# Column tiles with both high parts before both low parts, smaller memory claims and a shorter LayerNorm path in a two-layer hybrid trunk

## The chip, the cores and the metric

The kernel runs on one core of one Trainium2 chip. The metric is device time in microseconds (us), the median over several executions. Engines are named as in the profile: PE is TensorE (matmuls), PEld its weight load, DVE VectorE, ACT ScalarE, POOL GpSimd, SP the engine that issues most DMAs.

## What is computed

Two layers over 256 tokens of width 2048, then a final RMSNorm. Each layer normalises, projects to 14,848 columns at once, runs four token mixers of width 512 on their columns, and merges them:

```
h = rms_norm(x, norm_g)
proj = h @ w_in
ya = a_bg * depthwise_conv(a_cg * a_x, conv_a_w) * silu(a_z)          # A: 3 taps
yb = gqa_attention(axial_rope(rms_norm(q)), axial_rope(rms_norm(k)), v) * silu(b_z)   # B
yc = rwkv7_bidir(h, c_r, c_k, c_v, ...) * silu(c_z)                    # C: scan, both directions
u  = depthwise_conv(d_val * sigmoid(d_gate), dw_w) + dw_b              # D: 31 taps
yd = silu((u - mean(u)) * rsqrt(var(u) + LN_EPS) * ln_g + ln_b) * silu(d_z)
bp = einsum('bskc,kcd->bskd', stack([ya, yb, yc, yd]), w_branch)
x  = x + sum(sigmoid(gates + b_gate) * bp, branches) @ w_out
```

All arithmetic is float32. On PE a weight and an activation are each split into a rounded high part and a rest (low part), and a product is made of three passes: high x high, high x low and low x high.

## The kernel before

**Weights.** Per layer 306 chunks of 128x1024 float32 (512 KB) are streamed from memory into four `raw` buffers, one DMA each. From a chunk ACT makes its high part, `hi` (a rounding copy, `fetch`, line 423; three buffers), and DVE its low part, `lo` = raw - hi (`low`, line 437; two buffers). `chunk` (line 444) hands a chunk to PE and sees to it that three chunks are ahead in `hi` and two in `lo`; both copies are issued with high priority.

**Column tiles.** `tile_b` (line 478) makes 128 columns of a projection over all 256 tokens from two chunks. The activations stand in slabs as pairs (high | low) of 512 columns, so that one chunk takes 8 matmuls of 128x512 with `hi` (high x high and high x low side by side) and 8 of 128x256 with `lo`. Per chunk `wide` (line 467) issues the 8 with `hi`, then the 8 with `lo`; then comes the second chunk. A layer has 137 such tiles. `tile_branch` (line 488) does the same with one chunk for the branch outputs (32 per layer). Three PSUM buffers (`mg`) hold column tiles, one (`mb`) branch tiles, four (`sd`) the side work.

**Side work.** Normalising and the branches A to D are Python generators that run beside the stream of column tiles. A generator issues a few instructions and yields: a positive number is a delay on the planner's clock `k.now`; a negative one (`MM` -1.0, `PM` -1.5, `LN` -3.6) asks that its next matmul comes so many planner units after its operands are due. After each matmul of a column tile `pump` (line 352) issues the steps that are due, for each generator as far as its lead permits (`LEAD_A` 2.0, `LEAD_B` 1.8, `LEAD_D` 1.0), and so the place of a side matmul among PE's instructions is fixed when the program is built. PE, DVE and ACT each run their instructions in the order in which they were put, and wait where an operand is not there. The order on DVE and ACT is made by a scheduler, which puts `hi` and `lo` first where it can.

**Memory.** Side work takes its buffers from one arena. `room(words)` (line 279) holds a generator back until so many words are free beside what others have claimed. Branch B claims 2900 (line 712), branch C 3300 (line 839), 2400 (line 954) and 4300 (line 980).

**Branch D.** `conv_d` (line 758) adds the 31 taps on DVE, and `branch_d` (line 768) makes the LayerNorm: it adds the four 128-channel parts, sums them over channels on PE (the first sum), subtracts the mean on DVE and squares on ACT per part, adds the four squares, and sums again on PE (the second sum). The first sum is yielded as `LN`, the second as `MM`.

Where the text speaks of a part (`part`, `rounded`), a norm over heads or groups is meant: ACT rounds a value to `part`, DVE puts the rest beside it, and two PE matmuls sum both (`head_rstd`, line 664). Scan chunk means the steps of branch C's recurrence, whose small matrices ACT copies from PSUM (`bdE`, `bdR`, `bdS`).

Of the kernel before, what the change touches and what calls it, by code (L numbers as in the profile page):

```python
# [10 lines left out]
F32 = mybir.dt.float32  # L11
F32R = mybir.dt.float32r
AF = mybir.ActivationFunctionType
# [5 lines left out]
P = 128  # L19
D = 2048  # L20
S = 256
# [188 lines left out]


class Kern:
    AHEAD = 3
    FAR = 1
    INFL = 1.05
    RAW = 9
# [12 lines left out]
    LATE = 3.0  # L229
    LEAD_A = 2.0  # L230
    LEAD_B = 1.8
    LEAD_D = 1.0
    TAP = 1.0
    DMA = 2.5
    SLABS = 9
# [185 lines left out]
        return True  # L421

    def fetch(self):
        nc = self.nc
        while len(self.raws) < 1 + self.FAR and self.load():
            pass
        if not self.raws:
            return False
        raw = self.raws.pop(0)
        hi = self.wtile("hi", 3, F32R)  # L430
        with self.tc.high_priority():
            nc.scalar.activation(hi, raw, AF.Copy)
        self.ready.append([hi, None, raw])
        if self.tiles == 0 and len(self.ready) < 3:
            self.low(self.ready[-1])
        return True

    def low(self, w):

        if w[1] is None:  # L440
            w[1] = self.wtile("lo", 2, F32R)
            with self.tc.high_priority():
                self.nc.vector.tensor_tensor(w[1], w[2], w[0].bitcast(F32), ALU.subtract)

    def chunk(self):
        while len(self.ready) < self.AHEAD and self.fetch():
            pass
        w = self.ready.pop(0)
        self.low(w)
        if self.ready:  # L450
            self.low(self.ready[0])
        return w[:2]


    def passes(self, o, w, xs, first, last):
# [8 lines left out]
            nc.tensor.matmul(o, lo[:, c * P:(c + 1) * P], x[:, 0, :], start=False, stop=last and i == len(xs) - 1)  # L464
            self.pump()

    def wide(self, o, w, xs, first, last):

        nc = self.nc
        hi, lo = w  # L470
        for i, (c, x) in enumerate(xs):
            nc.tensor.matmul(o, hi[:, c * P:(c + 1) * P], x, start=first and i == 0, stop=False)
            self.pump()
        for i, (c, x) in enumerate(xs):
            nc.tensor.matmul(o[:, 0], lo[:, c * P:(c + 1) * P], x[:, 0, :], start=False, stop=last and i == len(xs) - 1)
            self.pump()

    def tile_b(self, src):


        self.tiles += 1
        o = self.psum(*(("mb", 1) if self.tiles == 4 else ("mg", 3))).rearrange("p (a t) -> p a t", a=2)
        for j in range(2):
            w = self.chunk()
            self.wide(o, w, [(k % 8, src[k // 4][:, k % 4]) for k in range(j * 8, j * 8 + 8)], j == 0, j == 1)
        return o

    def tile_branch(self, y):

        ps = self.psum("mb", 1)  # L490
        w = self.chunk()
        for j in range(2):
            self.passes(ps[:, j * S:(j + 1) * S], w, [(j * NT + k, y[:, k]) for k in range(NT)], True, True)
        return ps.rearrange("p (j t) -> p j t", j=2)

    def whole(self, out, ps):
# [196 lines left out]
    def branch_b(self, k, v, qz):  # L693
# [12 lines left out]
        for i in range(NT):  # L706
            while len(qz) <= i:
                yield 0.5
            q, bz = qz[i]
            if i == 0:  # L710
                ys = self.ys[1] = self.operand()
            yield from self.room(2900)
            rs = yield from self.head_rstd(q)
            qr = self.a1()
            yield from self.norm_rope(q, rs, self.pc("qg"), [(slice(0, P), qr)])
            self.f(q, rs)
            pt = self.a([P, 2, 2, S])
            pes = []
            for tb in range(2):
                ps = self.pside()  # L720
                nc.tensor.matmul(ps, qr[:, tb * P:(tb + 1) * P], kz.rearrange("p a t -> p (a t)"),
                                 start=True, stop=True)
                ps2 = ps.rearrange("p (a t) -> p a t", a=2)
                st = self.a([P, 6])
                nc.vector.tensor_reduce(st[:, 0:2], ps2, AX.X, ALU.max)
                nc.vector.tensor_scalar(st[:, 2:4], st[:, 0:2], -0.125, None, ALU.mult)
                pe = self.a([P, 2, S])
                for h in range(2):
                    nc.scalar.activation(pe[:, h], ps2[:, h], AF.Exp, scale=0.125, bias=st[:, 2 + h:3 + h],
                                         accum_out=st[:, 4 + h:5 + h])  # L730
                yield 0.5
                nc.vector.reciprocal(st[:, 4:6], st[:, 4:6])
                for h in range(2):
                    nc.scalar.activation(pe[:, h], pe[:, h], AF.Copy, scale=st[:, 4 + h:5 + h])
                self.f(st)
                pes.append(pe)
                yield 2 * self.MM
            self.f(qr)
            for tb, pe in enumerate(pes):
                ps = self.pside()  # L740
                for h in range(2):
                    for kb in range(2):
                        j = h * 2 + kb
                        nc.tensor.transpose(ps[:, j * P:(j + 1) * P], pe[:, h, kb * P:(kb + 1) * P], self.ident)
                self.f(pe)
                nc.scalar.activation(pt[:, :, :, tb * P:(tb + 1) * P],
                                     ps.rearrange("p (h k t) -> p h k t", h=2, k=2), AF.Copy)
                yield self.MM
            ps = self.pside()
            for kb in range(2):  # L750
                for h in range(2):
                    nc.tensor.matmul(ps[h * 64:h * 64 + 64, :S], vt[:, kb * P + h * 64:kb * P + h * 64 + 64],
                                     pt[:, h, kb, :], start=kb == 0, stop=kb == 1)
            self.f(pt)
            nc.vector.tensor_tensor(bz, ps[:, :S], bz, ALU.mult)
            self.finish(ys, i, bz)
            self.f(bz)
            yield 0.5
# [13 lines left out]
    def branch_d(self, acc, convs, dz):  # L772
# [6 lines left out]
            yield 0.5  # L779
        ys = self.ys[3] = self.operand()  # L780
        yield 0
        sq = self.a([P, NT, S])
        nc.vector.tensor_tensor(sq[:, 0:2], acc[:, 0:2], acc[:, 2:4], ALU.add)
        nc.vector.tensor_tensor(sq[:, 0], sq[:, 0], sq[:, 1], ALU.add)
        yield self.LN
# [1 line left out]
        nc.tensor.matmul(ps[:, :S], self.ones, sq[:, 0], start=True, stop=True)  # L787
        for i in range(NT):
            nc.vector.scalar_tensor_tensor(acc[:, i], ps[:, :S], -1.0 / W, acc[:, i], ALU.mult, ALU.add)
            nc.scalar.activation(sq[:, i], acc[:, i], AF.Square)  # L790
        nc.vector.tensor_tensor(sq[:, 0:2], sq[:, 0:2], sq[:, 2:4], ALU.add)
        nc.vector.tensor_tensor(sq[:, 0], sq[:, 0], sq[:, 1], ALU.add)
        yield self.MM
        ps = self.pside()
        made = nc.tensor.matmul(ps[:, :S], self.ones, sq[:, 0], start=True, stop=True)
        self.f(sq)
# [22 lines left out]
    def rwkv(self, rkv, tl, cz):  # L819
# [5 lines left out]
        for d in range(2):  # L825
# [8 lines left out]
            for p0 in range(0, NT, 2):  # L834
                pp = slice(p0, p0 + 2)
                v5 = lambda x: x.rearrange("p a (c t) -> p a c t", c=NCH)
                while self.cv < p0 + 1:
                    yield 0.5
                yield from self.room(3300)
                lbs = []  # L840
                for i in range(2):
                    lb = self.a([P, 2, P])
# [108 lines left out]
            self.cur.want = 0  # L951

            yield 4.0
            yield from self.room(2400)
            mb = self.a([P, 32, 32])
            for h in range(2):
                for b in range(2):
# [19 lines left out]
            nc.gpsimd.dma_start(scr2[1], xt[:64])  # L977
            self.f(xi, xt)
            self.cur.want = 0
            yield from self.room(4300)  # L980
            bd = self.bd
            ready = []
            self.add(self.inverses(bd, gs, scr2, ready))
# [534 lines left out]
```

## Time and profile before

| | |
|---|---|
| median of 3 runs | 1969.62 us (1969.13 to 1970.98) |
| profiled execution, its own time | 1970.32 us |
| its span (first to last instruction) | 1968.5 us |
| mean granted TensorE clock | 0.992 of full speed |
| PE busy | 1922.6 us (98%) |
| PEld busy | 1705.1 us (87%) |
| DVE busy | 1442.9 us (73%) |
| ACT busy | 1261.6 us (64%) |
| HBM traffic | 173 GB/s over the span |

The shares are averages over the whole span. The waits view lists per engine and operand how long the engine stood idle and which instruction released it; a row of the timeline is a run of like instructions, with its start, the time it took and, in brackets, the idle time before it. In the windows view PEclk is the mean granted clock of a stretch, as a share of full speed. Nearly all instructions bear line 201, the helper that records them; what they are is read from the names of output and inputs.

### The profile page before, as it was taken

To read this page: it belongs to the slowest core of one execution; us is meant where nothing else is said; L and a number is where in the kernel's file an instruction comes from. 1 tells how busy PE (TensorE), PEld (TensorE's weight loads), DVE (VectorE), ACT (ScalarE), POOL (GpSimd) and SP (SyncE) were. 2 spreads that over 40 slices of the span, in tenths; PEclk is the share of its full clock that TensorE was granted. 3 is DMA by queue.
4 is the path that set the end of the run, shared out by engine and by line. 5 is a ranking of instruction groups with operands and counts; after the bars stand their busy time and mean duration, and the time that the engine had idled before them with its cause. 6 is when DMAs were issued, how large, how long until landed. Compare 5 with 4: busy or idle time off the path is not lost.

```text
span 1968.5 us, 32326 instructions
## 1 busy us (share of the span) xinstructions
PE 1922.6 (98%) x12190; PEld 1705.1 (87%) x12190; DVE 1442.9 (73%) x2498; ACT 1261.6 (64%) x2292; POOL 71.3 (4%) x117
## 2 busy tenths in 40 slices
PE   8999999999999999999999999999999999999997
PEld 6888788899988998998888887889899899989886
DVE  7877869967787556666687778699777866565665
ACT  7777577667647776554567766766765577665544
POOL 2001010000001000000000011000001000000000
PEclk9999999999999999999999999999999999999998
DMA  7555453355565445566655555444555544455653
GB/s 256 182 178 171 148 161 136 135 178 184 169 198 171 148 152 190 188 203 215 210 191 182 169 174 165 136 142 151 179 173 186 174 166 151 149 188 195 218 183 128
DMA packets 97692, 343.17 MB, mean 174 GB/s; under 512 B 11808, under 2 KB 12192, under 8 KB 97536
## 3 DMA queue, kind: packets, MB, share of 16 engines
q1 hardware_dynamic: 93312, 331.48, 49.4%
q0 software_dynamic: 3648, 8.59, 1.8%
q8 instruction: 95, 1.56, 0.3%
q10 hardware_dynamic: 576, 1.05, 0.1%
q14 instruction: 61, 0.50, 0.1%
HBM read 332.48 MB, written 8.39 MB: 173 GB/s over the span
## 4 chain that ended last, share of the span: by engine, by line
PE 94%; DVE 4%; ACT 1%; issue 1%; DMA 0%; DVEq 0%; SPq 0%; ACTq 0%
PE mg L201 75%; PE mb L201 9%; PE sd L201 9%; DVE arena L201 2%; DVE lo L201 1%; ACT bdE L201 0%; ACT arena L201 0%; DMA arena<-xT 0%; ACT hi L201 0%; ACT L175 0%; DVE bdE L201 0%; DVE slab L201 0%; DVEq L1513 0%; ACT bdR L201 0%; ACT bdS L201 0%
## 5 line engine op out<-in xcount | busy, mean ns | idle before, releaser
L201 PE MATMUL mg<-slab,hi 128*128 128x512 f32 x4368 | 1135.3, 398 | 11.7 <-DVE slab L201 11.7
L201 DVE TENSOR_TENSOR lo<-raw,hi 128x1024 fp32r<-128x1024 f32 x612 | 748.6, 1223 | 352.2 <-PE mg L201 295.0
L201 ACT ACTIVATE hi<-raw 128x1024 fp32r<-128x1024 f32 x612 | 647.0, 1058 | 472.1 <-PE mg L201 311.8
L201 PEld LDWEIGHTS mg<-slab,hi 128*128 128x128 f32 x4368 | 783.9, 190 | 155.1 <-DVE slab L201 14.9
L201 PEld LDWEIGHTS mg<-slab,lo 128*128 128x128 f32 x4368 | 604.5, 191 | 47.7 <-issue 5.1
L201 PE MATMUL mg<-slab,lo 128*128 128x256 f32 x4368 | 640.3, 286 | 0.0
L201 DVE TENSOR_TENSOR arena<-arena 128x256 f32<-128x256 f32 (+18 forms) x392 | 166.9, 433 | 15.2 <-ACT arena L201 6.9
L201 DVE SCALAR_TENSOR_TENSOR arena<-arena,par 128x256 f32<-128x256 f32 x346 | 154.5, 483 | 4.7 <-ACT arena L201 3.7
L201 PE MATMUL mb<-slab,hi 128*128 128x256 f32 (+1 forms) x1040 | 152.9, 287 | 0.0
L201 DVE TENSOR_TENSOR arena<-mg,arena 128x256 f32<-128x256 f32 x305 | 127.8, 419 | 18.4 <-ACT arena L201 13.2
L201 PEld LDWEIGHTS mb<-slab,hi 128*128 128x128 f32 x1040 | 136.3, 191 | 0.9
L201 ACT ACTIVATE arena<-arena,b_gate 128x256 f32<-128x256 f32 x128 | 64.6, 505 | 73.8 <-DVE arena L201 73.2
L201 ACT ACTIVATE arena<-arena 128x256 f32<-128x256 f32 (+4 forms) x194 | 93.6, 498 | 25.7 <-DVE arena L201 24.8
L201 ACT ACTIVATE arena<-mg 128x256 f32<-128x256 f32 x241 | 89.3, 371 | 6.4 <-PE mg L201 3.7
L201 PE MATMUL mb<-slab,lo 128*128 128x256 f32 x528 | 87.7, 287 | 0.0
L175 ACT ACT_TABLE_LOAD x62 | 79.5, 1283 | 10.2 <-PE sd L201 7.7
L201 DVE SCALAR_TENSOR_TENSOR arena<-arena,mb 128x512 f32<-128x512 f32 x64 | 43.9, 686 | 55.4 <-PE mb L201 45.0
L201 PEld LDWEIGHTS mb<-slab,lo 128*128 128x128 f32 x528 | 73.6, 191 | 0.4
L201 ACT ACTIVATE bdE<-sd 64x128 f32<-64x128 f32 x256 | 62.9, 269 | 8.3 <-PE sd L201 5.8
L201 ACT ACTIVATE arena<-sd 128x64 f32<-128x64 f32 (+4 forms) x122 | 40.0, 330 | 21.9 <-PE sd L201 20.3
L201 ACT ACTIVATE arena<-arena,par 128x256 f32<-128x256 f32 x88 | 42.8, 508 | 5.5 <-DVE arena L201 4.2
L201 PE MATMUL sd<-arena 96*128 96x256 f32 (+3 forms) x224 | 43.7, 338 | 0.0
(96 smaller groups left out, 1019.5 us busy)
## 6 DMA issues: line engine op xcount, KB each, us to landing
raw<-w SPq DMA_DIRECT2D x612, 512.0 KB, 3.3
arena<-xT SPq DMA_DIRECT2D x4, 512.0 KB, 7.5
scratch<-slab POOLq DMA_DIRECT2D x16, 128.0 KB, 3.4
scratch<-arena POOLq DMA_DIRECT2D x8, 256.0 KB, 4.7
arena<-xT SPq DMA_DIRECT2D x8, 256.0 KB, 3.9
x<-arena SPq DMA_DIRECT2D x8, 256.0 KB, 4.8
arena<-x SPq DMA_DIRECT2D x8, 256.0 KB, 3.5
arena<-lorab POOLq DMA_DIRECT2D x16, 96.0 KB, 2.7
```

Of the source, the lines that this page charges most:

```text
L175: return f(out)
L201: return f(out, *args, **kw)
```

## The change

`tile_b` takes both chunks at its start. It issues the 8 matmuls with the first `hi`, the 8 with the second `hi`, then the 8 with the first `lo` and the 8 with the second. Copies for coming chunks are issued at fixed places: a `hi` after the eighth matmul and one at the tile's end, a `lo` after each eight low matmuls, with the DMA of a further `raw` behind it. `wide`, `AHEAD` and the loop in `chunk` go. `LEAD_D` goes from 1.0 to 1.4. The claims of `room` go from 2900 to 2400, 3300 to 3136, 2400 to 2304 and 4300 to 1500. In `branch_d` the buffer of the squares has two parts in place of four, each square is added to the sum as it comes, and the second sum is yielded as `LN`.

```diff
 class Kern:
-    AHEAD = 3
...
-    LEAD_D = 1.0
+    LEAD_D = 1.4
...
     def fetch(self):
-        nc = self.nc
-        while len(self.raws) < 1 + self.FAR and self.load():
-            pass
+
+        nc = self.nc
         if not self.raws:
-            return False
+            return
         raw = self.raws.pop(0)
         hi = self.wtile("hi", 3, F32R)
...
         if self.tiles == 0 and len(self.ready) < 3:
-            self.low(self.ready[-1])
-        return True
-
-    def low(self, w):
-
-        if w[1] is None:
-            w[1] = self.wtile("lo", 2, F32R)
-            with self.tc.high_priority():
-                self.nc.vector.tensor_tensor(w[1], w[2], w[0].bitcast(F32), ALU.subtract)
+            self.low()
+
+    def low(self):
+
+        for w in self.ready:
+            if w[1] is None:
+                w[1] = self.wtile("lo", 2, F32R)
+                with self.tc.high_priority():
+                    self.nc.vector.tensor_tensor(w[1], w[2], w[0].bitcast(F32), ALU.subtract)
+                self.load()
+                return
 
     def chunk(self):
-        while len(self.ready) < self.AHEAD and self.fetch():
-            pass
-        w = self.ready.pop(0)
-        self.low(w)
-        if self.ready:
-            self.low(self.ready[0])
-        return w[:2]
+        return self.ready.pop(0)[:2]
...
     def tile_b(self, src):
...
-        for j in range(2):
-            w = self.chunk()
-            self.wide(o, w, [(k % 8, src[k // 4][:, k % 4]) for k in range(j * 8, j * 8 + 8)], j == 0, j == 1)
+        ws = [self.chunk(), self.chunk()]
+        for k in range(KT):
+            c = k % 8
+            self.nc.tensor.matmul(o, ws[k // 8][0][:, c * P:(c + 1) * P], src[k // 4][:, k % 4], start=k == 0, stop=False)
+            self.pump()
+            if k == 7:
+                self.fetch()
+        for k in range(KT):
+            c = k % 8
+            self.nc.tensor.matmul(o[:, 0], ws[k // 8][1][:, c * P:(c + 1) * P], src[k // 4][:, k % 4, 0, :], start=False,
+                                  stop=k == KT - 1)
+            self.pump()
+            if c == 7:
+                self.low()
+        self.fetch()
         return o
...
     def tile_branch(self, y):
...
             self.passes(ps[:, j * S:(j + 1) * S], w, [(j * NT + k, y[:, k]) for k in range(NT)], True, True)
+        self.low()
+        self.fetch()
         return ps.rearrange("p (j t) -> p j t", j=2)
...
-            yield from self.room(2900)
+            yield from self.room(2400)
...
-        sq = self.a([P, NT, S])
+        sq = self.a([P, 2, S])
...
-            nc.scalar.activation(sq[:, i], acc[:, i], AF.Square)
-        nc.vector.tensor_tensor(sq[:, 0:2], sq[:, 0:2], sq[:, 2:4], ALU.add)
-        nc.vector.tensor_tensor(sq[:, 0], sq[:, 0], sq[:, 1], ALU.add)
-        yield self.MM
+            nc.scalar.activation(sq[:, int(i > 0)], acc[:, i], AF.Square)
+            if i:
+                nc.vector.tensor_tensor(sq[:, 0], sq[:, 0], sq[:, 1], ALU.add)
+        yield self.LN
...
-                yield from self.room(3300)
+                yield from self.room(3136)
...
-            yield from self.room(2400)
+            yield from self.room(2304)
...
-            yield from self.room(4300)
+            yield from self.room(1500)
```

Three places show what this does to the order. The first is PE at the first column tile (`mg` is the tile's PSUM buffer, the slabs are the four pieces of the normalised activations). Before:

```order
L201 MATMUL mg_209<-slab_106,hi_128 128x512 x4
L201 MATMUL mg_209<-slab_107,hi_128 128x512 x4
L201 MATMUL mg_209<-slab_106,lo_130 128x256 x4
L201 MATMUL mg_209<-slab_107,lo_130 128x256 x4
L201 MATMUL mg_209<-slab_108,hi_148 128x512 x4
L201 MATMUL mg_209<-slab_109,hi_148 128x512 x4
L201 MATMUL mg_209<-slab_108,lo_150 128x256 x4
L201 MATMUL mg_209<-slab_109,lo_150 128x256 x4
```

and now:

```order
L201 MATMUL mg_213<-slab_106,hi_128 128x512 x4
L201 MATMUL mg_213<-slab_107,hi_128 128x512 x4
L201 MATMUL mg_213<-slab_108,hi_150 128x512 x4
L201 MATMUL mg_213<-slab_109,hi_150 128x512 x4
L201 MATMUL mg_213<-slab_106,lo_130 128x256 x4
L201 MATMUL mg_213<-slab_107,lo_130 128x256 x4
L201 MATMUL mg_213<-slab_108,lo_152 128x256 x4
L201 MATMUL mg_213<-slab_109,lo_152 128x256 x4
```

The last slabs are read eight low matmuls earlier, and sixteen low matmuls follow them in place of eight.

The second is ACT around branch D's second sum in layer 2; the rows `arena<-arena 128x256` are the four squares, `bdR` and `bdE` copies of a scan chunk. Before:

```order
L201 ACTIVATE hi_15851<-raw_15800 128x1024
L201 ACTIVATE arena<-arena 128x256 x3
L201 ACTIVATE hi_15873<-raw_15849 128x1024
L201 ACTIVATE hi_15914<-raw_15871 128x1024
L201 ACTIVATE hi_15958<-raw_15912 128x1024
L201 ACTIVATE bdR_91<-rd 64x2x64 x2
L201 ACTIVATE bdE_83<-sd_15939 64x2x64 x8
L201 ACTIVATE arena<-arena 128x256
L201 ACTIVATE arena<-mg_15848 128x256
```

and now:

```order
L201 ACTIVATE hi_15806<-raw_15725 128x1024
L201 ACTIVATE arena<-arena 128x256 x2
L201 ACTIVATE arena<-mg_15744 128x256
L201 ACTIVATE arena<-arena 128x256
L201 ACTIVATE hi_15840<-raw_15737 128x1024
L201 ACTIVATE arena<-arena,b_gate_9958 128x256
L201 ACTIVATE arena<-arena 128x256
L201 ACTIVATE hi_15853<-raw_15792 128x1024
L201 ACTIVATE hi_15893<-raw_15804 128x1024
```

The fourth square stood behind a scan chunk's copies, which themselves wait for PE; now no such copy is ahead of it.

The third is DVE ahead of a `part` of branch B in layer 1, in the fifteenth column tile (`mg` rows empty a finished tile). Before:

```order
L201 TENSOR_TENSOR lo_993<-raw_937,hi_966 128x1024
L201 TENSOR_TENSOR slab_670<-arena 128x8x64
L201 SCALAR_TENSOR_TENSOR arena<-arena,par_71 128x256 x2
L201 TENSOR_TENSOR lo_1019<-raw_964,hi_991 128x1024
L201 TENSOR_TENSOR arena<-mg_963,arena 128x256
L201 MEMSET arena 128x8
L201 TENSOR_TENSOR part_1023<-arena,part_1023 128x512
L201 TENSOR_TENSOR lo_1044<-raw_989,hi_1017 128x1024
```

and now:

```order
L201 TENSOR_TENSOR lo_1007<-raw_903,hi_972 128x1024
L201 SCALAR_TENSOR_TENSOR arena<-arena,par_71 128x256 x2
L201 TENSOR_TENSOR lo_1019<-raw_918,hi_985 128x1024
L201 TENSOR_TENSOR arena<-mg_976,arena 128x256
L201 TENSOR_TENSOR part_996<-arena,part_996 128x512
L201 SCALAR_TENSOR_TENSOR slab_682<-arena,derived_191 128x256
```

The two `lo` in front of the `part` are now those whose buffers come free at the end of the tile before, 0 and 8 low matmuls from its end, and the two matmuls that read the `part` stand behind the fifth `hi` matmul of tile 15, where they stood behind its twenty-third matmul.

## Rows read from the trace of the kernel before

**Rows 1.** Page, part 1: busy time, share of the span and instructions of each engine.

```profile
PE 1922.6 (98%) x12190; PEld 1705.1 (87%) x12190; DVE 1442.9 (73%) x2498; ACT 1261.6 (64%) x2292; POOL 71.3 (4%) x117
```

**Rows 2.** Waits of PE: operand and its maker, us in total, times, longest.

```profile
PE mg L201 <- DVE slab L201: 11.7, 5, 8.6
PE sd L201 <- DVE arena L201: 7.8, 6, 4.9
PE sd L201 <- ACT part L201: 6.6, 2, 3.8
PE sd L201 <- DVE part L201: 3.8, 2, 1.9
PE sd L201 <- ACT bdE L201: 1.9, 1, 1.9
```

**Rows 3.** Windows: us, busy of each engine (instructions), PEclk, DMA share, GB/s.

```profile
224.40:231.20 6.80, 5.49 (x17) 4.69 (x18) 5.56 (x15) 5.21 (x8) 0.00 (x0) 0.50 0.13 52
...
1193.80:1197.20 3.40, 3.14 (x8) 2.49 (x9) 3.16 (x9) 2.25 (x4) 0.00 (x0) 0.50 0.26 99
...
345.00:350.00 5.00, 3.12 (x18) 2.52 (x17) 5.00 (x12) 3.19 (x5) 0.00 (x0) 1.00 0.32 107
```

**Rows 4.** Timeline of PE, two chunks of steady work in the output projection.

```profile
905.03 2.00 PE L201 MATMUL mg<-slab,hi 128*128 128x512 f32 x8
906.87 1.12 PE L201 MATMUL mg<-slab,lo 128*128 128x256 f32 x8
907.83 2.00 PE L201 MATMUL mg<-slab,hi 128*128 128x512 f32 x8
```

**Rows 5.** Groups by form: xcount, busy us, mean ns, idle before; DVE's `lo`, tap, tile, add.

```profile
L201 DVE TENSOR_TENSOR lo<-raw,hi 128x1024 fp32r<-128x1024 f32 x612 | 748.6, 1223 | 352.2 <-PE mg L201 295.0 <-ACT hi L201 19.7 <-issue 18.3
L201 DVE SCALAR_TENSOR_TENSOR arena<-arena,par 128x256 f32<-128x256 f32 x346 | 154.5, 483 | 4.7 <-ACT arena L201 3.7
L201 DVE TENSOR_TENSOR arena<-mg,arena 128x256 f32<-128x256 f32 x305 | 127.8, 419 | 18.4 <-ACT arena L201 13.2 <-PE mg L201 4.0
L201 DVE TENSOR_TENSOR arena<-arena 128x512 f32<-128x512 f32 x84 | 59.3, 710 | 7.0 <-ACT arena L201 6.9
...
L201 DVE TENSOR_TENSOR part<-arena,part 128x512 fp32r<-128x512 f32 x24 | 16.5, 688 | 4.3 <-ACT part L201 4.3
```

**Rows 6.** Timeline, PE at first tiles: of the program, tile 9, projection, layer 2.

```profile
16.55 1.11 PE L201 MATMUL mg<-slab,lo 128*128 128x256 f32 x8
...
17.50 2.00 PE L201 MATMUL mg<-slab,hi 128*128 128x512 f32 x8
...
67.49 0.73 PE L201 MATMUL mg<-slab,hi 128*128 128x512 f32 x2 [0.54 <-DVE slab L201]
...
895.12 0.74 PE L201 MATMUL mg<-slab,hi 128*128 128x512 f32 x2 [0.59 <-DVE slab L201]
...
986.47 0.50 PE L201 MATMUL mg<-slab,hi 128*128 128x512 f32 x1 [1.45 <-DVE slab L201]
```

**Rows 7.** Timeline, branch D's LayerNorm: first sum, scan adds, second sum of layer 1; layer 2.

```profile
588.93 0.70 PE L201 MATMUL sd<-arena,consts 128*128 128x256 f32 x2 [0.71 <-DVE arena L201]
...
596.80 1.83 DVE L201 TENSOR_TENSOR arena<-arena 64x175 f32<-64x175 f32 x5
...
600.37 0.70 PE L201 MATMUL sd<-arena,consts 128*128 128x256 f32 x2 [1.01 <-DVE arena L201]
...
1565.90 2.01 ACT L201 ACTIVATE bdE<-sd 64x128 f32<-64x128 f32 x8
...
1571.01 1.22 PE L201 MATMUL sd<-arena,consts 128*128 128x256 f32 x2 [4.91 <-DVE arena L201]
```

**Rows 8.** Timeline, PE at two `part` sums and at a scan chunk.

```profile
103.54 0.62 PE L201 MATMUL sd<-part,rounded 128*128 128x512 f32 x2
...
225.71 1.04 PE L201 MATMUL sd<-part,rounded 128*128 128x256 f32 x2 [3.83 <-ACT part L201]
...
362.49 0.49 PE L201 MATMUL sd<-arena,bdE 128*128 128x128 f32 x2 [1.87 <-ACT bdE L201]
```

More of the change, by code (lines that the diff above doesn't have):

```diff
@@ L465, in passes @@
             self.pump()
-    def wide(self, o, w, xs, first, last):
-        nc = self.nc
[L470 to L476, printed above, removed]
     def tile_b(self, src):
```

## The prediction, made before the changed kernel was run

> **What bounds the kernel now.** I read four views in this order. The page's engine line comes first [rows 1]: PE is busy for 1922.6 us of a span of 1968.5, so whatever the change does to DVE (73%) or ACT (64%) counts only where PE is kept waiting. PE's idle time is 45.9 us. Second, PE's waits [rows 2]: 31.8 us stand in five groups. 8.6 of the first group is the start of the program; the other 23.2 us are side work that PE reached before its operand: a late slab of activations, a sum of branch D, a `part`, a scan chunk. No `hi` and no `lo` stands there, so weights are never late. Third, the clock: four stretches are granted 1.2 instead of 2.4 GHz, two of 6.8 us and two of 3.4 (one of each in [rows 3]), each during or behind a stall of PE; 20.4 us at half speed lose at most 10.2 us. A stretch with 1.88 us of idle PE, from 345 to 350, kept its full clock [rows 3]. Fourth, steady work [rows 4]: eight `hi` matmuls take 1.84 us (0.23 each), eight `lo` matmuls 0.96 (0.12 each), and a chunk's end and the next chunk's start leave nothing between them.
>
> The ceiling of any gain is thus some 23 us of stalls and 10 us of clock, 33 us or 1.7%. A measurement of this kernel can tell about 0.2% (3.9 us) from no change.
>
> **The change part by part.** *Order of the matmuls.* The same matmuls in number and size run in another order. Since going from `hi` to `lo` and back is free in [rows 4], I cost the reorder itself at nothing. A cost or gain at such a switch would show in 548 places fewer than before (two of four switches in each of 274 tiles); the rows bound it to under 0.01 us at each, 5 us either way.
>
> *Weights.* A `lo` buffer now comes free 0.96 us before a tile's end and another at its end. The first is needed after the next tile's sixteen `hi` matmuls, 16 x 0.23 = 3.7 us later than the tile's start, so 4.65 us in all, of which the pair takes 2 x 1.22 [rows 5]. Some 2.2 us are left for the work that stands ahead on DVE, four taps (0.48) or so. The work of the pair is hidden by the `hi` matmuls; if that cover goes, see the third rival. `raw` DMAs are issued once a `lo` is out, with a whole tile to land. Cost nothing.
>
> *Late slabs.* Where the last slab of activations is what PE waits for, sixteen low matmuls are left behind it instead of eight: 8 x 0.12 = 0.96 us more. This holds at the program's first tile (low matmuls from 16.55, next tile at 17.50 [rows 6]; +0.96) and at layer 2's first tile (a wait of 1.45 becomes 2.4; +0.96). At the start of each layer's output projection (wait 0.59) DVE has no `lo` ahead of the split, which gives half of it back: +0.5 twice. In tile 9 (0.54) the split now ends about 2.5 us after the tile before (0.2, a `lo` 1.22, an emptied tile 0.42, the split 0.69), and PE wants it after 14 x 0.23 = 3.2: that wait goes. Sum +0.96 + 0.96 + 1.0 - 0.54 = **+2.4**.
>
> *Branch D's LayerNorm.* The second sum is asked for later and its last square no longer stands behind a scan chunk's eight copies (2.01 us) on ACT; the 1.01 us of layer 1 and the 4.91 of layer 2 [rows 7] go: -5.9. The first sum gets worse in layer 1. In the new order DVE has, after the end of the tile before, 0.5 us of the first `lo`, a scan add of 0.37 (five took 1.83 [rows 7]), the second `lo` 1.22, a tile's emptying 0.42, seven scan adds 2.6, and the adds of the sum, 0.71 and 0.42 [rows 5], with another scan add of 0.35 between: 6.6 us. PE is there after 16 x 0.23 + 2 x 0.12 = 3.9 us: 2.7 us late, in layer 2 by the like sum 0.4. For such sums made over DVE's queue of before, at the places where PE's wait was measured, I found 0.63 of the sum to be real, so I take 1.7 + 0.3 = 2.0 against the 0.71 of before: +1.3. Together **-4.6**.
>
> *Norms over heads and groups.* Four waits for a `part` cost 10.4 us before (6.6 + 3.8 [rows 2], the longest in [rows 8]). Because the two `lo` now come as a pair, the places change. In tile 15 PE did not wait before (103.54 [rows 8]); now DVE has 0.5 us of the first `lo`, two taps 0.96, the second `lo` 1.22, a tile's emptying 0.42 and the `part`'s rest 0.69 [rows 5], 3.8 us after the tile's end, while PE is there after six `hi` matmuls, 1.4 us: 2.4 us late. The same sum gives 2.3 in tile 30, 3.2 at the query norm of layer 1 (3.83 now), 0.8 in tile 36, 2.3 in tile 51, and 3.6 and 1.9 at two places of layer 2: 16.5 us, of which 0.63 is 10.4. The bounds are no change at all and +6.1; I take **+1.0**, near the calibrated end.
>
> *Scan chunks.* One wait of 1.87 us before [rows 8]; by the same sums two now, 2.6 and 3.6 us, of which 0.63 is 3.9: **+2.0**, bounds +1 to +4.
>
> *Claims and `LEAD_D`.* They let branches start sooner, and the order shows side matmuls moved by about a tile, with 7 to 12 taps to a tile as before. The taps lie beside PE's work, on a DVE that idles for 27% of the time. Nothing by itself; what it does is in the places above.
>
> *Clock.* Of the four stretches layer 2's at the second sum (6.8 us) goes. New stalls of 2 us and more can bring others. I count five of 3.4 us, 17.0 us against 20.4, half of the difference: **-1.7**, bounds -7 and +5 (one stretch of 3.4 us costs 1.7).
>
> Sum: +2.4 - 4.6 + 1.0 + 2.0 - 1.7 = -0.9 us, on the profiled execution's 1970.3 us (span 1968.5 and 1.8 around it): 1969.4. That execution lies 0.7 us above the median of the runs, so the forecast is **1968.7 us**, no change that can be told. Its own range, from the bounds above, is 1962 to 1976.
>
> **The rivals.** *First, faster.* DVE is asked for `lo` once a tile and not twice, and the planner, with smaller claims and more lead, has more steps at hand, so that what PE reaches too early thins out everywhere and not in the LayerNorm alone. For it: DVE waits 295 us for PE to free a `lo` buffer [rows 5], and during such a wait nothing behind it runs; half as many such waits let steps go earlier. Against it: the tile 15 sum. If the 23.2 us of stalls halve (-11.6) and the stretches at half clock with them (-5.1), with +2.4 at the first tiles kept: 1970.3 - 0.7 - 14.3 = **1955 us**.
>
> *Second, slower.* The pair of `lo` at the head of DVE's queue makes every short step behind it later by one more `lo`, 1.22 us. It decides at the places where PE has less than 2.4 us of room behind the pair, that is, for side matmuls among the first ten of a tile's `hi` matmuls (10 x 0.23). The profile for it: `part` and first-sum waits as worked out above for tile 15 and layer 1. Against it: a side matmul that sits later in a tile has 3.7 us and more. Eight such places more than I count are 8 x 1.22 = 9.8 us, and three further stretches of 3.4 us at half clock 5.1: 1968.7 + 14.9 = **1984 us**. The Trainium skill has the rule on its page "Perfetto Trace Analysis", section "Optimizing Scalar/DVE Operations": where a vector engine is not saturated but causes bubbles on others, breaking up its work lets pieces finish sooner. Putting the two `lo` together is the reverse of that; by that rule it is this rival that comes true, and the trace of before agrees so far that DVE at 73% leaves PE waiting.
>
> *Third, slower by late weights.* If DVE's work ahead of the pair exceeds the 2.2 us left in a quarter of the 274 tiles by 0.2 us, PE waits for `lo` for 68 x 0.2 = 14 us: 1983 us. Against it: no wait for `lo` before, with the same 4.65 us.
>
> *Fourth, it does not do what it says:* the claims and leads move no step that PE waits for. That is the forecast with other small terms, and counted there.
>
> **How the numbers follow.** The forecast has 0.46, the first rival 0.29, the second 0.21, the third 0.04. The range should reach into both sides: from 1953, below the first rival's time, to 1984, the second's: left out are about half of the slower rivals, a third of the first, and little of the forecast's own, some 0.2. Against the median of 1969.6, faster by over 0.2% means below 1965.7, slower above 1973.5. Of the forecast's 0.46 I put 0.08 below, 0.07 above and 0.31 between; of the first rival 0.27 below; of the slower ones 0.23 above, and the few hundredths left lie between: 0.35, 0.35 and 0.30.
>
> **What would show it.** Right: PE's waits have the DVE arena group at about 3 us, the `part` groups near 11, the slab group at 14; no `lo` among PE's waits; DVE's wait for PE ahead of `lo` in fewer and longer pieces; four to six half-clock stretches of mostly 3.4 us. The steps would be wrong if the second sums still wait (LayerNorm), if `part` waits vanish or double (the 0.63), or if PE waits for `lo` (the weights). The prediction is wrong if stalls in the middle fall below 15 us or rise above 32.

## The result, and the profile after

| | before | after |
|---|---|---|
| median, lowest and highest (4 runs each) | 1969.70 us (1969.13 to 1970.98) | 1982.90 us (1980.44 to 1988.17) |
| ratio | | 1.0067, 95% interval 1.0055 to 1.0079 |
| profiled execution; its span | 1970.32; 1968.5 us | 1981.06; 1979.1 us |
| PE, DVE, ACT busy | 1922.6, 1442.9, 1261.6 us | 1922.3, 1439.0, 1277.3 us |

The change makes the kernel 13.2 us slower, where no change was forecast (1968.7 us). The time lies inside the range, at its slow end; that end was put at 1984 us for the slower rivals, so that the range holds the time owes nothing to the forecast's own sum, whose range ended at 1976. PE does the same work in the same time; it waits more. PE's waits after (operand and its maker, us in total, times, longest):

```profile
PE mg L201 <- DVE slab L201: 15.0, 6, 8.7
PE mb L201 <- ACT slab L201: 6.4, 2, 4.9
PE sd L201 <- ACT part L201: 5.8, 4, 2.3
PE sd L201 <- DVE arena L201: 4.9, 2, 2.5
PE sd L201 <- DVE part L201: 4.0, 5, 1.2
PE mb L201 <- DVE lo L201: 3.9, 5, 1.6
PE sd L201 <- ACT arena L201: 2.2, 3, 1.0
PE sd L201 <- ACT bdE L201: 1.5, 1, 1.5
PE sd L201 <- ACT bdS L201: 0.6, 2, 0.4
```

They sum to 44.3 us; before it was 31.8 in the five groups of [rows 2] and 1.6 in two small ones. The difference, 10.9 us, is the difference of the spans, 10.6. (The medians differ by 2.6 us more; of that no trace was kept.) Two groups are new, both with `mb`, the branch tiles: a slab from ACT (6.4) and a `lo` (3.9). The places, from the timeline after (start, us, engine, operation; idle time before it in brackets):

```profile
13.61 3.66 PE L201 MATMUL mg<-slab,hi 128*128 128x512 f32 x8 [1.44 <-DVE slab L201]
...
102.90 0.50 PE L201 MATMUL sd<-part,rounded 128*128 128x512 f32 x1 [0.91 <-ACT part L201]
...
104.31 0.50 PE L201 MATMUL sd<-part,rounded 128*128 128x512 f32 x1 [0.91 <-DVE part L201]
...
590.89 0.70 PE L201 MATMUL sd<-arena,consts 128*128 128x256 f32 x2 [2.43 <-DVE arena L201]
...
1318.52 4.84 DVE L201 SCALAR_TENSOR_TENSOR arena<-arena,par 128x256 f32<-128x256 f32 x12
...
1324.55 0.62 PE L201 MATMUL mb<-slab,lo 128*128 128x256 f32 x3 [1.61 <-DVE lo L201]
...
1335.12 0.46 PE L201 MATMUL sd<-arena,bdE 128*128 128x128 f32 x2 [2.46 <-DVE arena L201]
...
1573.52 0.59 PE L201 MATMUL sd<-arena,consts 128*128 128x256 f32 x2
1574.16 1.28 ACT L175 ACT_TABLE_LOAD   x1
...
1583.34 0.48 ACT L201 ACTIVATE arena<-sd,eps 128x256 f32<-128x256 f32 x1
...
1602.22 0.87 PE L201 MATMUL mb<-slab,hi 128*128 128x256 f32 x2 [1.52 <-ACT slab L201]
...
1607.93 0.43 DVE L201 SCALAR_TENSOR_TENSOR slab<-arena,slab 128x256 fp32r<-128x256 f32 x1 [0.48 <-ACT slab L201]
1607.95 1.26 PE L201 MATMUL mb<-slab,hi 128*128 128x256 f32 x3 [4.86 <-ACT slab L201]
```

Rows of before to compare them with, from its timeline (a scan chunk, the rsqrt of layer 2, the last slab of branch D):

```profile
1330.25 0.46 PE L201 MATMUL sd<-arena,bdE 128*128 128x128 f32 x2 [0.72 <-DVE arena L201]
...
1573.56 0.47 ACT L201 ACTIVATE arena<-sd,eps 128x256 f32<-128x256 f32 x1
...
1594.80 0.42 DVE L201 SCALAR_TENSOR_TENSOR slab<-arena,slab 128x256 fp32r<-128x256 f32 x1
```

The sum of layer 2 at 1573.52 no longer waits, where it waited 4.91 us [rows 7]. But the rsqrt on ACT (`arena<-sd,eps`) starts 9.6 us behind it (2.0 before; here and below from the start of the second of the sum's two matmuls), the four parts of branch D's end take 25.0 us from there to the last slab (21.7 before), and PE, which reads them in its branch tile, stands 1.52 us until ACT has made the second and 4.86 us until it has made the last. The wait has moved from the sum to its consumer. The granted clock (windows view; us, busy of PE, PEld, DVE, ACT and POOL, PEclk, DMA share, GB/s):

```profile
15.10:18.50 3.40, 3.40 (x12) 2.88 (x12) 1.23 (x4) 3.40 (x5) 0.00 (x0) 0.50 1.02 406
233.50:236.90 3.40, 3.40 (x14) 3.05 (x14) 2.99 (x9) 3.36 (x4) 0.00 (x0) 0.50 0.02 5
591.90:595.30 3.40, 3.40 (x19) 3.40 (x18) 3.40 (x9) 1.28 (x4) 0.00 (x0) 0.50 0.00 0
1336.00:1339.40 3.40, 3.40 (x16) 3.11 (x14) 3.40 (x8) 0.68 (x3) 0.00 (x0) 0.50 0.01 2
1605.70:1612.50 6.80, 4.55 (x20) 4.38 (x21) 2.18 (x6) 2.20 (x7) 0.00 (x0) 0.50 0.45 149
```

20.4 us at 1.2 GHz, as long as before, at other places, each behind or within a stall of PE (the end of the span, where PE has no more work, is left out in both). PE is busy for 18.2 us of them, 17.1 before, so that the clock explains at most some 0.5 us of the loss of this execution. In some of the experiments it explains more.

### The profile page after: what moved, and what is told of

Its sections match the earlier page's. It is cut to its first block, busy times and chain, and to the rows that moved or that the text cites. A ratio compares the mean times of both kernels' runs of the same rounds, so it can differ in the third digit from the quotient of the medians.

```text
span 1979.1 us, 32423 instructions
## 1 busy us (share of the span) xinstructions
PE 1922.3 (97%) x12190; PEld 1708.2 (86%) x12190; DVE 1439.0 (73%) x2500; ACT 1277.3 (65%) x2294; POOL 71.0 (4%) x117
## 4 chain that ended last, share of the span: by engine, by line
PE 88%; DVE 5%; ACT 2%; issue 2%; DMA 2%; POOL 0%; DVEq 0%; SPq 0%; POOLq 0%; ACTq 0%
PE mg L201 71%; PE mb L201 9%; PE sd L201 9%; DVE arena L201 3%; DVE lo L201 2%; ACT hi L201 1%; ACT arena L201 1%; DMA raw<-w 1%; DMA arena<-scratch 1%; ACT bdE L201 0%; DMA scratch<-slab 0%; DVE slab L201 0%; POOL arena L201 0%; DMA arena<-xT 0%; ACT slab L201 0%
## 5 line engine op out<-in xcount | busy, mean ns | idle before, releaser
L201 PE MATMUL mg<-slab,hi 128*128 128x512 f32 x4368 | 1095.5, 397 | 15.0 <-DVE slab L201 15.0
L201 PEld LDWEIGHTS mg<-slab,hi 128*128 128x128 f32 x4368 | 795.7, 189 | 171.5 <-DVE slab L201 18.0
L201 DVE TENSOR_TENSOR lo<-raw,hi 128x1024 fp32r<-128x1024 f32 x612 | 735.7, 1221 | 251.4 <-PE mg L201 194.3
L201 PE MATMUL mg<-slab,lo 128*128 128x256 f32 x4368 | 598.5, 287 | 0.0
L201 PEld LDWEIGHTS mg<-slab,lo 128*128 128x128 f32 x4368 | 569.1, 192 | 25.4 <-issue 4.5
L201 DVE TENSOR_TENSOR arena<-arena 128x512 f32<-128x512 f32 (+17 forms) x394 | 166.7, 431 | 34.2 <-ACT arena L201 22.9
L201 DVE SCALAR_TENSOR_TENSOR slab<-arena,slab 128x512 fp32r<-128x512 f32 (+1 forms) x64 | 35.5, 555 | 26.2 <-ACT slab L201 26.0
```

The source lines that it names most:

```text
L201: return f(out, *args, **kw)
```

## The experiments

Each was timed against the kernel before on the same chip, whose median there lay between 1970.6 and 1971.3 us (1969.70 beside the change itself); ratios are to it. Two experiments compared with each other can come from two chips, so that a difference of 1 to 2 us between them says little. "The order" is that of the matmuls in a column tile. Where a profiled execution spends longer at half clock, PE is busy for longer with the same matmuls; then the difference of two spans is split into PE's idle time and its busy time. The place of a side matmul is the number of tile matmuls that stand before it among PE's instructions in the trace.

**e1, the order alone**, with its fixed places for the copies (claims, `LEAD_D` and `branch_d` as before).

> The kernel before with the new order of matmuls alone (claims, lead and LayerNorm as before). Theory A (two late operands at branch tiles: branch D's last slab in layer 2, 6.4 us, and a `lo`, 3.9 us; the slab is late because the rsqrt of the LayerNorm stands behind other work on ACT): in this order the rsqrt stands right behind its sum, so the slab wait is absent or under 1 us, the `lo` waits of about 4 us and some 3 us more at the first tiles stay, and the old waits at the second sum may come back: 1975 to 1979 us. Theory B (the pair of `lo` makes every short step later; the order is the whole loss): 1983 us. Theory C (claims and lead are the loss): 1970 to 1973 us.

Measured: 1989.16 us, 1.0098 (1.0084 to 1.0112). PE's waits:

```profile
PE mb L201 <- ACT slab L201: 16.1, 4, 7.9
PE mg L201 <- DVE slab L201: 15.3, 6, 9.1
PE mb L201 <- DVE lo L201: 3.8, 4, 3.2
```

The order alone costs more than the whole change. Of the 21.8 us by which its profiled execution is longer than that of before, 14.8 are idle time of PE and 7.0 busy time, with 34.1 us at half clock (20.4 before). Branch D's slab is late in layer 1 here (11.7 of the 16.1 us), with the rsqrt only 4.9 us behind its sum; theory A named the place but not the cause.

**e2, all but the order** (the kernel before with the new claims, `LEAD_D` 1.4 and the new `branch_d`).

> The change without the new order of matmuls: smaller claims, lead 1.4 and the shorter LayerNorm on the kernel before. Theory A: no `lo` waits and old first tiles; the second sums of the LayerNorm no longer wait (about 6 us less), but the rsqrt of layer 2 stands behind other work on ACT here too, so up to 6 us of a slab wait can come: 1964 to 1971 us. Theory B: only the gain of the LayerNorm is left, 1964 us. Theory C: the loss is here, 1978 us or more.

Measured: 1967.48 us, 0.9986 (0.9977 to 0.9995): faster by 0.14%, less than the bound of 0.2%. Claims and lead are not the loss.

**e3, the rsqrt's buffer early.**

```diff
         sq = self.a([P, 2, S])
+        rs = self.a1()
...
         self.f(sq)
-        rs = self.a1()
```

> The changed kernel with one buffer taken earlier: the result of the LayerNorm's rsqrt gets its memory together with the squares, not after the second sum. Theory A: the rsqrt goes right behind the sum on ACT, branch D's slab is there in time, the 6.4 us slab wait of PE and the half-clock stretch behind it (6.8 us) go: 7 to 10 us less, 1973 to 1976 us. Theories B and C: within 2 us of the changed kernel, as the order of matmuls and the claims are untouched.

Measured: 1985.51 us, 1.0077 (1.0064 to 1.0090). The rsqrt now starts 1.7 us behind its sum, and PE still waits 5.1 us for branch D's slabs (6.4): the four parts behind it take 30.7 us. PE's side matmuls stand at the same places as in the change, so nothing was moved on PE. Theory A's cause falls.

**e4, branch tiles: high matmuls first.** Both halves' sixteen, then the eight low ones, in one accumulation group.

> The changed kernel with the sixteen high matmuls of a branch tile first and its eight low ones last (they came as 8, 4, 8, 4). `lo` is then wanted 0.96 us later. Theory A: PE's waits for `lo` fall from 3.9 us to under 1.5 us, 2.5 to 4 us less than the changed kernel, the slab wait stays: 1978 to 1980 us. Theories B and C: within 2 us of the changed kernel.

Measured: 1981.79 us, 1.0058 (1.0045 to 1.0072). The aimed wait is gone, another came:

```profile
PE sd L201 <- DVE arena L201: 8.6, 3, 3.1
...
PE mb L201 <- DVE lo L201: 0.2, 1, 0.2
```

3.7 us of waits for `lo` on branch tiles and 4.1 for their slabs went, and 3.7 more at DVE's sums and 1.7 for `lo` at column tiles came. The gain of the median, 1.1 us, is within the spread of the runs.

**e5, the old order in the changed program** (`hi` issued at the change's places; a `lo` and the load behind it, as in the change, after each eight low matmuls, of which the first eight now come in the middle of the tile).

```diff
+        each = True
         for k in range(KT):
+            if k == 8 and each:
+                for i in range(8):
+                    self.nc.tensor.matmul(o[:, 0], ws[0][1][:, i * P:(i + 1) * P], src[i // 4][:, i % 4, 0, :], start=False, stop=False)
+                    self.pump()
+                self.low()
...
-        for k in range(KT):
+        for k in range(8 if each else 0, KT):
```

> The changed kernel with the matmuls of every column tile in the old order (high, low, high, low), while `hi`, `lo` and the DMA of a further chunk are still issued at the fixed places of the change. Theory B (with the new order both `lo` come at a tile's end as a pair on DVE, and what stands behind it in DVE's and ACT's queues is late): like the change without the new order, 1966 to 1970 us, and ACT's waits for a chunk's DMA under 10 us. Theory C' (the fixed places are the loss: a further chunk is loaded only behind a `lo`, lands late, and ACT stands waiting for it): 1978 to 1984 us, ACT's waits for a chunk's DMA 50 us or more.

Measured: 1967.84 us, 0.9985 (0.9976 to 0.9994), ACT's waits for a chunk's DMA 5.7 us. With e2 this shows that the fixed places of the copies cost nothing in the old order (0.4 us), and that the loss, some 15 us, comes with the new one. It does not part two things that come together in the new order: PE's matmuls stand otherwise, and the first `lo` of a tile and the load behind it are issued later. A kernel in the new order with its loads issued earlier was not run; e15 and e16 give a price for late loads.

**e6 and e7, the old order only in the merge stretch, and the new one only there** (`each` true for tiles 50 to 121 of a layer, and for the others).

> The changed kernel with the old order of matmuls in the column tiles of the merge stretch alone (72 of 137 in a layer, those among which the branch tiles lie), the new order elsewhere. Theory B with the place of theory A (branch D's tail and the branch tiles' `lo`): PE's waits at branch tiles go, the first tiles' 3 us stay: 1969 to 1973 us. If the loss is spread over all tiles: half of it stays, 1976 to 1978 us.

> The reverse: the new order in the merge stretch alone, the old one elsewhere. Theory B with that place: the waits at branch tiles stay and the first tiles are as before, 1976 to 1981 us. If the loss is spread: 1975 us. If it lies in the tiles outside the merge: 1969 us or less.

Measured: 1985.15 us, 1.0076 (1.0064 to 1.0089), and 1977.08, 1.0029 (1.0018 to 1.0039). The two losses against e5, 17 and 9 us, sum to far more than the whole. In e6 PE's waits at branch tiles fell to 1.4 us, but those for `arena` results of DVE are 16.6 us where the change has 4.9. So the loss can't be cut by places in this way. The traces show why the two halves don't add: the planner places the side matmuls anew where the order changes. In tiles 1 to 49 of both layers e6 has all 787 side matmuls where the change has them, and e7 all 812 where e5 has them. In the merge stretch of layer 1, 504 of e6's 559 stand at places that neither the change nor e5 has.

**e8, `lo` in halves** (two instructions of 128x512, four buffers of half the size).

> The changed kernel with each `lo` made as two instructions of 512 columns in buffers of half the size, so that a buffer comes free after four low matmuls and DVE's longest piece is half as long (some 0.65 us each, about 50 us more work on DVE in all). Theory B: the work left on DVE at a tile's end falls from about 1.9 us to 1.2, PE's waits at branch tiles fall by a third or more: 1974 to 1980 us. Theory C': the further chunk is still loaded behind a whole `lo`, no gain, 1983 us or more.

Measured: 1989.95 us, 1.0095 (1.0079 to 1.0110). DVE's half `lo` takes 685 ns, so DVE has 54 us more work (789.6 us for `lo` against 735.7), and PE waits 21.1 us for slabs at branch tiles. The Trainium skill ("Perfetto Trace Analysis", "Optimizing Scalar/DVE Operations") says that breaking up instructions may let work complete sooner, where an engine that isn't saturated causes bubbles on others. This run shows no gain from it; the added work on DVE is in this run too, so the two are not told apart. Of the 8.6 us by which its profiled execution is longer than the change's, 7.1 are busy time of PE, with 40.8 us at half clock.

**e9, the first tiles in the old order** (`each` for the first tile of each layer and of each projection).

> The changed kernel with the old order of matmuls in four column tiles alone, the first of each layer and the first of each output projection. If the late slabs there cost what the traces show between tile starts (2.1, 1.0, 0.5 and 0.5 us against before): 4 us less than the changed kernel, 1979 us. If the loss at the first tiles only moves: within 1 us of it.

Measured: 1981.20 us, 1.0046 (1.0034 to 1.0058). PE's slab wait falls from 15.0 to 11.6 us, as long as before; the median gains 1.7, half of it, which lies within the spread of both kernels. No side matmul of PE moved in this run.

**e10, branch D's tail first** (e3, and the tail's steps at high priority).

> The changed kernel with the rsqrt's buffer taken early (as in the third run) and the twenty-eight steps of branch D's tail, from the rsqrt to its last slab, put ahead of other work on DVE and ACT where the scheduler can. Theory T (the tail is late at its branch tile, because the new order stretches it from 20 to 22 us to 24 us and more, on a DVE that is busy all through it): PE's waits for an ACT slab at branch tiles fall under 1.5 us, some 5 us less than the third run, 1978 to 1981 us. If the tail's place in the queues is not what delays it: within 2 us of the third run, 1985 us.

Measured: 1984.94 us, 1.0070 (1.0056 to 1.0084). Slab waits 5.6 us, the tail still 30.6 us in layer 2. The scheduler's priority did not shorten it.

**e11, e2 with the rsqrt's buffer early.**

> The change without the new order of matmuls (the second run), with the rsqrt's buffer taken early. In the second run the rsqrt of layer 2 came 12.1 us after its sum, and PE waited 2.9 us at branch D's first tile. Theory T: that wait goes, 2 to 5 us less than the second run, 1963 to 1966 us. Otherwise within 1 us of it.

Measured: 1961.23 us, 0.9950 (0.9937 to 0.9962), the fastest kernel of the study, ahead of both, and 1.8 us below what theory T gave. PE's waits:

```profile
PE mg L201 <- DVE slab L201: 12.0, 5, 8.9
PE sd L201 <- ACT part L201: 6.6, 2, 3.8
PE sd L201 <- DVE arena L201: 5.0, 2, 3.8
PE sd L201 <- ACT bdS L201: 1.2, 5, 0.3
PE sd L201 <- DVE part L201: 1.1, 1, 1.1
PE sd L201 <- ACT arena L201: 1.0, 1, 1.0
PE sd L201 <- issue: 0.4, 1, 0.4
```

No wait at a branch tile is left. In the old order the rsqrt's buffer was a cause: PE's matmuls stand at the same places as in e2, and the rsqrt of layer 2, 12.1 us behind its sum there and 2.0 here, no longer waits for DVE. In e2 it started 0.2 us behind three scan adds; that its result had been given memory that they still used is read from this and from the edit.

**e12, all mends in the new order** (e4, e9, e10 together).

> The changed kernel with all mends together: the tail of branch D ahead, the rsqrt's buffer early, the branch tiles' high matmuls first, the first tiles in the old order. If the losses add (4 us at the first tiles, 4 to 6 at branch tiles' `lo`, 5 to 8 at branch D's slab): 1966 to 1971 us. If a mended wait comes back elsewhere: 1975 us or more.

Measured: 1980.21 us, 1.0048 (1.0036 to 1.0060). The mends give 2.7 us together, within the spread of the change's runs; 4.6 us of slab wait stand at branch D's tile, now in layer 1, and DVE's sums wait 10.8.

**e13, e14, e17, e18, the distance of the two `lo`** (in e5's edit `k == 10`, 13, 14, 15 in place of 8).

> The changed kernel with the first eight low matmuls of each column tile after ten high ones, six high and then the other eight low behind them, so that the two `lo` buffers come free 6 x 0.23 + 8 x 0.12 = 2.3 us apart (2.8 in the old order, where 1967.8 us was measured; 0.96 in the new, 1982.9). Theory B: 1968 to 1972 us, PE's waits at branch tiles under 3 us.

> The same with the first eight low matmuls after thirteen high ones: 3 x 0.23 + 8 x 0.12 = 1.65 us apart. Theory B: between the old and the new order, 1972 to 1979 us. If the time does not follow the distance (1983 us or more here, or 1968), B is not the whole.

> The changed kernel with the first eight low matmuls of each column tile after fourteen high ones: the two `lo` buffers come free 2 x 0.23 + 8 x 0.12 = 1.42 us apart, more than the 1.22 us of one `lo`. Theory B with a threshold: 1964 to 1972 us, as at 1.65. Theory S: anywhere from 1962 to 1985 us.

> The same after fifteen high ones: 0.23 + 0.96 = 1.19 us apart, less than one `lo`. Theory B with a threshold: 1976 to 1985 us, near the changed kernel. Theory S: anywhere from 1962 to 1985 us.

Measured, with the two ends:

| between the two `lo` buffers coming free | median | ratio (interval) | ACT waits for a chunk's DMA |
|---|---|---|---|
| 2.8 us (old order, e5) | 1967.84 | 0.9985 (0.9976 to 0.9994) | 5.7 |
| 2.3 (e13) | 1977.15 | 1.0036 (1.0023 to 1.0048) | 4.9 |
| 1.65 (e14) | 1965.70 | 0.9975 (0.9967 to 0.9984) | 26.4 |
| 1.42 (e17) | 1976.33 | 1.0028 (1.0019 to 1.0037) | 30.1 |
| 1.19 (e18) | 1986.61 | 1.0066 (1.0052 to 1.0080) | 36.9 |
| 0.96 (new order, the change) | 1982.90 | 1.0067 (1.0055 to 1.0079) | 64.4 |

Below the length of one `lo` (1.22 us) both kernels are slowest; above it the four scatter over 11.5 us without order, and e13 and e17 lie outside what theory B gave for them. That fits a threshold with a scatter on top, and the scatter is nearly as large as the step, so the threshold is not shown by itself. Two things in the traces weaken it further. Of the 14.1 us between the spans of e17 and e18 only 4.3 are idle time of PE; 9.8 are busy time, with 37.4 us at half clock in e18 and 17.0 in e17. And with the distance the planner moves the side steps: 1298 of PE's 1886 side matmuls stand at other places in e18 than in e17. Seven further kernels in the new order (e1, e3, e4, e8, e9, e10, e12) lie between 1980 and 1990; the four in the old one (before, e2, e5, e11) between 1961 and 1971.

**e15 and e16, one raw buffer fewer** in the new and the old order (`FAR` 0, the arena unchanged).

> The changed kernel with three buffers for raw chunks in place of four (the memory of the fourth left unused). Theory R: ACT's waits for a chunk's DMA rise from 64 to 150 us or more, and the time by 10 us or more, 1993 us. Theory B: within 4 us of the changed kernel, as long as no `hi` is late for PE.

> The old order of matmuls with the rest of the change (the fifth run), with three buffers for raw chunks. Theory R: ACT waits 50 us or more for a chunk's DMA, and the time rises towards the changed kernel, 1975 to 1983 us. Theory B: within 3 us of the fifth run, 1966 to 1971 us.

Measured: 2015.32 us, 1.0239 (1.0220 to 1.0258), and 1976.11, 1.0035 (1.0023 to 1.0048). ACT's waits for a chunk's DMA, of the change, of e15 and of e16:

```profile
ACT hi L201 <- DMA raw<-w: 64.4, 74, 2.4
```

```profile
ACT hi L201 <- DMA raw<-w: 438.1, 370, 5.0
```

```profile
ACT hi L201 <- DMA raw<-w: 256.1, 191, 3.5
```

PE waits only 2.6 us for a `hi` in e15 and not at all in e16, yet both get slower, with PE's side matmuls (all but 2) at the same places as without the edit. The reading is that ACT, standing at a `hi` that nobody needs yet, holds the side steps behind it: PE's waits for `part`, `arena`, `bdS`, `bdE` and `slab` from ACT are 28.7 us in e15 and 16.5 in the change. 250 us more of such waits cost e16 8.3 us against e5, 374 more cost e15 32 against the change. By these rates the 59 us that the change adds over e5 are worth 2 to 5 of its 15 us (an estimate from e5, e15 and e16, which takes the cost as going with the waits).

## Why the prediction was wrong

The forecast failed at terms that it put at nothing. By its own sign it is wrong as well: stalls in the middle are 35.6 us (44.3 without the start's 8.7), above the 32 that it named.

- **Order of the matmuls, "I cost the reorder itself at nothing": a step that failed.** For PE alone this held in the change: its busy time is the same within 0.3 us. As a price of the order it failed: alone it costs 18.6 us (e1), and without it the rest gains 3.1 (e2).
- **Weights, "4.65 us in all ... Cost nothing": a step that failed.** The window was worked out for column tiles. A branch tile behind one wants its `lo` after eight high matmuls of 128x256, 0.96 us, so the window is 0.96 + 0.96 = 1.9 us, of which a `lo` takes 1.22. It was missed at 5 of 64 branch tiles, 3.9 us; at the longest (1.61 at 1324.55) DVE had twelve taps, 4.84 us, ahead of the `lo`.
- **"`raw` DMAs ... with a whole tile to land. Cost nothing": failed.** They land late for ACT 74 times, 64.4 us (3.4 before); PE never waits for that, but side steps on ACT do, at an estimated 2 to 5 us (e15, e16).
- **LayerNorm: its end a step that failed.** The sums themselves came as said: the second ones no longer wait, and the first of layer 1 waits 2.43 us (2.7 by the queue, 1.7 taken after the factor 0.63). What failed is the end of the sum, "-4.6": I stopped at the second sum and did not say what is late next. It was the tail behind it, at branch D's tile: +6.4 us. At the sums themselves -4.2 came of the -4.6.
- **Late slabs:** +2.4 said, +3.3 measured (11.7 to 15.0): the program's first tile cost 1.6 where 0.96 was said, by a new wait of 1.44 at 13.61 and a start 0.2 later, and tile 9 gave back 0.35 of 0.54. **Norms:** +1.0 said, -0.6 measured (10.4 to 9.8), tile 15 with 1.8 us where 2.4 was worked out. **Scan chunks:** +2.0 said, +1.4 measured (1.9 + 0.7 to 1.5 + 2.5); the 0.7, at 1330.25 before, stood in the `arena` group of [rows 2], and the prediction did not count it. **Clock:** 17.0 us at half clock said, -1.7; 20.4 measured, so nothing. These terms sum to -0.1 where the forecast has -0.9; what the sum lacked were the branch tiles, +10.3 us, and small waits, +0.7.
- **The rivals.** The second (slower, 1984 us) is nearest in time. Its mechanism, a pair of `lo` that delays short steps on DVE, fits the two slowest distances, but e13 and e17 lost some 9 us against e5 with the pair apart, and most of the step from e17 to e18 is time at half clock. The third, waits for `lo`, came true at branch tiles with 3.9 us.

What stays open: no run gives back most of the 15 us of the order while it keeps the order. Taking away single waits gave back 1.1 and 1.7 us (e4, e9), and all of them together 2.7 (e12), where other waits came. Shown are that the loss comes with the order, the waits of the change's own trace, which account for the 10.6 us of its profiled execution, and that late loads have a price. How much of the rest is the nearness of the two `lo`, how much the later loads and how much the new places of side steps (1856 of 1886 side matmuls stand elsewhere in e5 than in the change), these runs don't tell. In the old order new places alone cost little: e2 and e5 differ in 1089 of them and by 0.4 us.

## What to carry to other kernels

When a change shortens a window for copies, work the window out for every kind of tile that follows, and count the engines that stand at a copy in order, not only PE. When a wait disappears from the sum, follow its operand to the next consumer: the wait may stand there. Where a planner places side work, a change of order redraws nearly all of it in the stretch where the order changes; separate it from the rest of an edit before judging either, as the half without the order, with one buffer taken early, was the better kernel (e11).

## What the runs showed that was not expected

Some kernels in the new order also vary more from run to run: 1980.2 to 1989.6 us (e10, 6 runs) and 1980.4 to 1988.2 (the change), against 1960.4 to 1962.0 (e11, 5 runs) and 1966.7 to 1969.1 (e2, 11 runs). Not all do: e8 lies between 1988.9 and 1990.1 (4 runs). The clock has a part in it. In e10 the mean granted clock of an execution falls from 0.994 in the fastest to 0.990 in the slowest, which is worth some 8 of the 9.4 us between them (an estimate, 0.004 of 1985 us); in the change it falls only from 0.993 to 0.992 for 7.7 us. They are also those whose ACT waits for DMAs; that the one makes the other was not tested.
